# A transformer block on one core: late modulation columns summed on VectorE, two gates' products moved into the latent attention, rotary keys' low part on 128 rows

## The chip, the core and the metric

One Trainium2 chip, one of its cores. The metric is the device time of one execution in microseconds (us), the median of several runs. The engines are TensorE (PE: products into PSUM; PEld is its loading of weights), VectorE (DVE), ScalarE (ACT), GpSimd (POOL) and SyncE (SP), whose queue issues nearly all weight transfers. PSUM has eight banks of 128 x 512 floats.

## The reference

One layer on 256 latent rows `x` and 256 context rows, width 1024, all in float32. Cut to what matters here:

```python
m = silu(c) @ ada_w + ada_b                  # 6 x 1024 columns, split in six
h = rms_norm(x, g1) * (1 + m[1]) + m[0]
z = h @ w_in                                 # retention q, k, v, gate; latent cq, ckv, kr; gates g_ret, g_mla
att = softmax((q_nope @ k_nope + rope(q_rope) @ rope(k_rope)) * scale) @ v    # 8 heads
ret = bidirectional_retention(rope(q), rope(k), v)                            # 4 heads
r = head_rms(ret) * silu(ret_gate)
merged = sigmoid(g_ret) * (r @ w_branch_ret) + sigmoid(g_mla) * (att @ w_branch_mla)
x = x + m[2] * (merged @ w_out)
h2 = rms_norm(x, g2) * (1 + m[4]) + m[3]
x = x + m[5] * moe(h2)                       # top 4 of 32 experts, clamped SwiGLU
out = rms_norm(x, final_g)
```

`m[0]` and `m[1]` are needed at the start. The late modulation columns are `m[2]` to `m[5]`, 4096 columns of `ada_w`, needed only after the two branches are merged.

## The kernel before, in words

The program is a list of steps (`step`), which one Python pass turns into instructions in the order of the list; each engine takes its own in that order. A step may name a weight tile: 128 partitions x 1024 floats, 512 KB, loaded by SP into a ring of `WR` = 10 places, each refilled when it has been read. Most tiles are split into two float32r halves, high and low, in `split` (ScalarE copies, L276; VectorE subtracts, L277) `AHEAD` = 2 steps before their use, and a product is then three matmuls in `mm3` (L285 to L287). A raw tile is used as it is.

The stages in order: `ada_half` computes `m[0]`, `m[1]`; `modulate` gives the rows `hh`, `hl`; the latent projections; four pairs of heads of latent attention; `w_branch_mla`; four retention heads; the merge and `w_out`; the router; the experts. For each pair of heads the attention goes through `kv_up`, `scores` (the low part of the rotary keys, `krl`, has 64 rows, L700), the softmax on VectorE and ScalarE (L704 to L711), `attend_rows` (16 transposes, then four splits whose VectorE part is `ptl` and `kn`, L282), `q_rot` for the next pair, and `attend`. Between them stand steps that have work for TensorE meanwhile.

The late modulation columns are two quarters `q` of 2048 columns, eight steps `k` each (`ada_step`, L328 to L342). A step multiplies two raw tiles with a 128 x 32 stationary in four column groups; the first of a quarter also adds the bias (L296), and the bank of the quarter stays taken until its last step. Quarter 0 is spread over the attention by `FILL`, quarter 1 over the retention heads, two steps each. The gate columns of the attention (`C_GM + 512`) are four steps in pairs 1 to 3, the gate of a retention head (`C_RG + 512 * h`) four steps behind its scores. `gates` (L1154) spreads the sums over all rows for the residual and turns others into columns for the second modulation.

The expert weights, 192 transfers of 2 MB, pass through nine slots: three opened in `open_ring` in the last retention head, one in `close_early`, and at the end of the dense stage four rings (`add_ring(RINGS[2], ...)`) in the memory of `wr`, `wp` and `fk`, and one more, `halves`.

Of the kernel before, what the change touches and what calls it, by code (L numbers as in the profile page):

```python
# [21 lines left out]
TA = 512  # L22
# [7 lines left out]
RINGS = 3, 1, 4, 1  # L30
WR = 10
AHEAD = 2
FILL = 0, 1, 2, 1, 1, 1, 1, 1
MID = 4
# [25 lines left out]
def hybrid_block(ctx: ExitStack, tc: tile.TileContext, A, out, dbg=None):  # L60
# [21 lines left out]

    front = ExitStack()
    wr = [enter(front, f"wr{i}") for i in range(WR)]
    wp = [enter(front, f"wp{i}") for i in range(AHEAD + 1)]
    fk = enter(front, "fk")
    accp = enter(ctx, "accp", side="right")
# [17 lines left out]
    x0 = sp.tile([128, 4, D], F32, name="x0")  # L105
    adab = fk.tile([12, 512], F32, name="adab")
    dec = fk.tile([128, 2, RH], F32, name="dec")
# [30 lines left out]
    nc.vector.memset(magic, 0x5f3759df)  # L138
    pick = fk.tile([128, 128], F32, name="pick")
    nc.gpsimd.memset(pick, 0.0)  # L140
    for g in range(4):
        nc.gpsimd.memset(pick[32 * g:32 * g + 1], 1.0)
    slot = cst.tile([128, CAP], F32, name="slot")
# [38 lines left out]
    transpose(rp[:, 0:16], crow)  # L182
    sT = fk.tile([128, KD, 32], F32, name="sT")
    nc.vector.memset(sT, 0.0)
    nc.vector.tensor_copy(sT[:, :, 0:2], rp[:, 0:16].rearrange("p (r k) -> p k r", r=2))
    cols = fk.tile([128, 21], F32, name="cols")
# [15 lines left out]
    ada0 = sp.tile([128, 512], F32, name="ada0")  # L202
    ada = fk.tile([128, 2, 512], F32, name="ada")
    mod1 = fk.tile([128, 2, 2, KD], F32, name="mod1")
# [122 lines left out]

    def ada_step(q, k):  # L328

        for i in range(2):  # L330
            def f(w, i=i):
                if k == 0 and i == 0:
                    bank("ada")
                for c in range(2):
                    g = 2 * i + c
                    o = B["ada"][32 * g:32 * g + 32]
                    if k == 0:
                        ada_bias(o, 4 * (q + 1) + g)
                    nc.tensor.matmul(o, sT[:, k], w[:, 512 * c:512 * c + 512], start=False, stop=(k == KD - 1))  # L339
                if k == KD - 1 and i == 1:  # L340
                    nc.scalar.activation(ada[:, q], B["ada"], AF.Copy)
            step(f, (A["ada_w"][0], 128 * k, 1, [(2048 * (q + 1) + 1024 * i, 1024)], True))  # L342
# [60 lines left out]
    def whole(p):  # L403
        return p

    def project_lat(c0, names, kks=range(4)):
# [84 lines left out]
    def open_mla():  # L491
        dump("mod1", mod1)
        nc.sync.dma_start(tabm, A["tables"][:, 1024:1536])

        for q in range(4):
            nc.sync.dma_start(bgu[32 * q:32 * q + 32], A["exp_b_gu"][0, :, 512 * q:512 * q + 512])
        start.close()
        M["mp"] = enter(mla, "mp", reuse_waits="tile")
        M["mp2"] = enter(mla, "mp2", 2, reuse_waits="tile")
        mp = M["mp"]  # L500
        M["mT"] = [p.tile([128, MH, T], F32R, name="w") for p in first]
        M["cq"] = [mp.tile([128, 3, T], F32R, name=n) for n in ("cqh", "cql")]
        M["ck"] = [mp.tile([128, 2, TA], F32R, name=n) for n in ("ckh", "ckl")]
        M["krh"] = mp.tile([128, TA], F32R, name="krh")
        M["krl"] = mp.tile([64, TA], F32R, name="krl")
        M["acc"] = accp.tile([128, 2, D], F32, name="acc_m")
# [6 lines left out]
    def cq_norm():  # L513
        open_mla()
        mp = M["mp"]
# [172 lines left out]
    def scores(pair):  # L688
# [3 lines left out]
        for t in range(2):  # L692
# [48 lines left out]
    q_up(0, range(1, 3))  # L741
    npair = MH // 2
    for pair in range(npair):
        kv_up(pair)
# [6 lines left out]
        if pair == 1:  # L751
            q_up(1, range(2, 3))
            project_lat(C_GM + 512, ("gm0", "gm1"), range(1))
        if pair == 2:
            project_lat(C_GM + 512, ("gm0", "gm1"), range(1, 2))
        n = sum(FILL[:2 * pair])
        for k in range(FILL[2 * pair]):
            ada_step(0, n + k)
        if pair == 3:
            project_lat(C_GM + 512, ("gm0", "gm1"), range(2, 4))  # L760
            step(lambda: gate_mla_out(1))
# [43 lines left out]
    for c in range(2):  # L805
        step(lambda: bank("bm0", "bm1"))
        for k2 in range(4):
            matmul2(("bm0", "bm1"), "w_branch_mla", 256 * k2, 512 * c, lambda: M["mT"], 2 * k2, k2 == 0, k2 == 3)
        step(lambda c=c: branch_mla_out(c))

# [136 lines left out]

    def gate_out():
        sg = R["qe"].tile([128, 2, 512], F32, name="sg")
        for t in range(2):  # L950
            pg = B[("pg0", "pg1")[t]]
            tg = R["qe2"].tile([128, 512], F32, name="tg")
            nc.scalar.activation(tg, pg, AF.Tanh, scale=0.5)
            nc.vector.scalar_tensor_tensor(sg[:, t], tg, 1.0, pg, op0=OP.add, op1=OP.mult)
        R["sg"] = sg


# [17 lines left out]
    def ret_norm(h):  # L975
# [7 lines left out]
        for t in range(2):  # L983
            r = R["qp2"].tile([128, 512], F32, name="r")
            nc.vector.scalar_tensor_tensor(r, B[("po0", "po1")[t]], ro[:, t:t + 1], R["sg"][:, t],
                                           op0=OP.mult, op1=OP.mult)
# [16 lines left out]
    for h in range(RH):  # L1003
# [14 lines left out]
        else:  # L1018
# [20 lines left out]
        step(lambda: against_rows(1))  # L1039
        values(h, 0)  # L1040
        step(lambda: against_rows(2))
        values(h, 1)
        step(lambda: against_rows(3))
        if h == RH - 1:
# [109 lines left out]
    def gates():  # L1154
        mod2, rw, rbias = O["mod2"], O["rw"], O["rbias"]
        for i in range(2):
            s = slice(32 * i, 32 * i + 32)
            ps = pt_()
            nc.tensor.matmul(ps, pick[s], ada[s, 0], start=True, stop=True)
            nc.scalar.activation(O["gate1"][i], ps, AF.Copy)  # L1160
        ps = pt_()
        for i in range(2):
            s = slice(32 * (2 + i), 32 * (2 + i) + 32)
            nc.tensor.matmul(ps[64 * i:64 * i + 64], pick[s, 0:64], ada[s, 1], start=True, stop=True)
        nc.scalar.activation(O["gate2"], ps, AF.Copy)
        for q in (1, 0):
            pc = pt_((128, 4, 4, 32))
            for c in range(4):
                transpose(pc[:, c].rearrange("p a b -> p (a b)"), pairs(ada[:, q], 2)[:, c // 2, c % 2])
            for g in range(2):  # L1170
                if q == 1:
                    nc.vector.scalar_tensor_tensor(mod2[:, 0, 4 * g:4 * g + 4], pc[:, :, g, 0], 1.0,
                                                   g2c[:, 4 * g:4 * g + 4], op0=OP.add, op1=OP.mult)
                else:
                    nc.vector.tensor_copy(mod2[:, 1, 4 * g:4 * g + 4], pc[:, :, 2 + g, 0])

# [509 lines left out]
```

## Time and profile before

| | us |
|---|---|
| median of 3 runs | 1508.16 (1507.0 to 1508.19) |
| the profiled execution's own time | 1507.75 |
| its span, first to last instruction | 1506.0 |
| PE busy | 1414.9 (94%) |
| DVE busy | 613.6 (41%) |
| ACT busy | 345.8 (23%) |
| POOL busy | 77.0 (5%) |
| bytes moved | 492.38 MB, 327 GB/s over the span |

The page of the profile has the busy time of each engine, the span in 40 slices of 37.65 us, the chain of waits that ended last, and the costliest groups of instructions. The trace behind it is asked for single stretches, engines and lines. A busy TensorE says only that products follow each other, since they are pipelined: what one costs is read from the distance of two starts. An engine's idle time costs something only where another one waits for it.

### The profile page before, as it was taken

The numbers are of one execution on the slowest core, as the hardware profiler recorded it, in microseconds if no ns is written. First come the engines' busy times: TensorE is split into PE (matmuls) and PEld (weight loads), VectorE is DVE, ScalarE is ACT, GpSimd is POOL, SyncE is SP. The second block draws the span as 40 slices with busy tenths as digits, with TensorE's granted clock in tenths as the row PEclk, the third lists the DMA queues.
The fourth block names the chain that finished last, engine by engine and source line by source line (L and its number), as shares of the span: only waits on it lengthen the run. The fifth ranks groups of instructions, "written<-read, shape, count | busy, mean of one in ns | idle before, by whom it ended". The sixth has DMA issues, their size and how long they took to land.

```text
span 1506.0 us, 19151 instructions
## 1 busy us (share of the span) xinstructions
PE 1414.9 (94%) x7979; PEld 771.2 (51%) x7979; DVE 613.6 (41%) x1080; ACT 345.8 (23%) x606; POOL 77.0 (5%) x98
## 2 busy tenths in 40 slices
PE   8999999999999998999999999989899889998885
PEld 4676787888887884333333333333333333333323
DVE  4485645556576565232332323322232223223223
ACT  4363443444344341111010010110010001001101
POOL 2100040101010012000000000000000000000000
PEclk9999999999999999999999999999999999999998
DMA  9634363353546948999999999999999999999994
GB/s 319 203 109 144 140 227 108 128 192 112 182 126 210 352 166 369 426 426 427 426 428 425 429 425 427 428 425 429 426 427 426 428 427 428 426 427 427 427 422 178
DMA packets 75046, 492.38 MB, mean 327 GB/s; under 512 B 6563, under 2 KB 16860, under 8 KB 50120
## 3 DMA queue, kind: packets, MB, share of 16 engines
q1 hardware_dynamic: 74008, 489.22, 80.6%
q0 software_dynamic: 544, 1.21, 0.3%
q8 instruction: 64, 1.05, 0.3%
q10 hardware_dynamic: 400, 0.66, 0.1%
q14 instruction: 30, 0.25, 0.0%
HBM read 490.02 MB, written 1.05 MB: 326 GB/s over the span
## 4 chain that ended last, share of the span: by engine, by line
PE 55%; DMA 38%; DVE 5%; ACT 1%; issue 1%; POOL 0%; ACTq 0%; DVEq 0%; SPq 0%
DMA w<-in_exp_w_gu_dram 25%; DMA w<-in_exp_w_down_dram 13%; PE ps L1451 11%; PE ps L285 9%; PE ps L287 9%; PE ps L286 9%; PE ps L1482 5%; PE ps L149 3%; PE ps L1312 1%; PE ps L308 1%; PE ps L339 1%; PE ps L296 1%; PE ps L1431 1%; PE ps L437 1%; DVE up L1459 1%
## 5 line engine op out<-in xcount | busy, mean ns | idle before, releaser
L1451 PE MATMUL ps<-w,xg 128*64 128x512 f32 x2048 | 460.1, 596 | 38.1 <-DMA w<-in_exp_w_gu_dram 36.0
L1451 PEld LDWEIGHTS ps<-w,xg 128*64 128x64 f32 x2048 | 140.6, 137 | 336.0 <-issue 251.6
L1482 PE MATMUL ps<-w,ga 128*64 128x512 f32 x992 | 218.1, 592 | 0.0
L277 DVE TENSOR_TENSOR ws<-w,ws 128x1024 fp32r<-128x1024 f32 (+2 forms) x114 | 138.8, 1224 | 72.6 <-ACT ws L276 71.5
L1438 DVE SCALAR_TENSOR_TENSOR x<-ps,gate,x 128x512 f32<-128x512 f32 x124 | 84.5, 744 | 188.4 <-PE ps L1431 188.4
L1482 PEld LDWEIGHTS ps<-w,ga 128*64 128x64 f32 x992 | 71.3, 137 | 141.6 <-issue 141.6
L276 ACT ACTIVATE ws<-w 128x1024 fp32r<-128x1024 f32 (+2 forms) x114 | 116.9, 1027 | 94.5 <-PE ps L287 83.0
L1491 DVE TENSOR_TENSOR ps<-ps,gate 128x512 f32<-128x512 f32 (+1 forms) x33 | 22.5, 683 | 268.6 <-PE ps L1482 259.6
L1456 ACT ACTIVATE ps<-ga 128x512 f32<-128x512 f32 x32 | 19.3, 602 | 473.7 <-DVE ga L1455 473.7
L286 PE MATMUL ps<-ws,hh 128*128 128x512 f32 (+3 forms) x304 | 108.8, 358 | 3.2 <-DVE ws L277 3.2
L287 PE MATMUL ps<-ws,hl 128*128 128x512 f32 (+3 forms) x304 | 108.7, 357 | 0.7 <-DVE hl L384 0.7
L285 PE MATMUL ps<-ws,hh 128*128 128x512 f32 (+3 forms) x304 | 109.3, 360 | 0.0
L1455 DVE TENSOR_SCALAR ga<-ps 128x512 f32<-128x512 f32 x32 | 22.1, 691 | 162.4 <-PE ps L1451 162.4
L281 ACT ACTIVATE up<-ps 128x512 fp32r<-128x512 f32 (+1 forms) x33 | 19.3, 584 | 259.0 <-DVE ps L1491 258.9
L286 PEld LDWEIGHTS ps<-ws,hh 128*128 128x128 f32 x304 | 57.1, 188 | 12.8 <-DVE ws L277 4.6
L285 PEld LDWEIGHTS ps<-ws,hh 128*128 128x128 f32 x304 | 57.1, 188 | 12.7 <-issue 4.4
L1312 PE MATMUL ps<-bgu,ident 128*64 128x512 f32 x256 | 62.0, 605 | 0.0
L287 PEld LDWEIGHTS ps<-ws,hl 128*128 128x128 f32 x304 | 57.1, 188 | 8.5 <-DVE hl L384 1.0
L149 PE MATMUL ps<-ident,up 128*128 128x128 f32 x128 | 23.8, 308 | 22.9 <-DVE up L1459 22.9
L1398 PE MATMUL ps<-oh,acc_m 128*128 128x128 bf16 x512 | 40.1, 222 | 0.0
L1471 ACT ACTIVATE ga<-ps 128x512 f32<-128x512 f32 x32 | 19.1, 597 | 74.5 <-PE ps L149 74.5
L287 PE MATMUL ps<-ath,htl 128*128 128x256 f32 x128 | 35.8, 280 | 0.0
(382 smaller groups left out, 1812.2 us busy)
## 6 DMA issues: line engine op xcount, KB each, us to landing
w<-in_exp_w_gu_dram SPq DMA_DIRECT2D x124, 2048.0 KB, 39.1
w<-in_exp_w_down_dram SPq DMA_DIRECT2D x62, 2048.0 KB, 39.1
w<-in_ada_w_dram SPq DMA_DIRECT2D x48, 512.0 KB, 4.5
w<-in_w_in_dram SPq DMA_DIRECT2D x48, 512.0 KB, 4.7
w<-in_w_in_dram SPq DMA_DIRECT2D x32, 256.0 KB, 5.3
w<-in_w_branch_ret_dram SPq DMA_DIRECT2D x16, 512.0 KB, 5.4
w<-in_exp_w_gu_dram SPq DMA_DIRECT2D x8, 1024.0 KB, 27.1
w<-in_w_branch_mla_dram SPq DMA_DIRECT2D x8, 512.0 KB, 4.7
```

Of the source, the lines that this page charges most:

```text
L149: nc.tensor.transpose(dst, src, ident[:n, :n])
L276: nc.scalar.activation(hi[:, :n], src, AF.Copy)
L277: nc.vector.tensor_tensor(lo[:, :n], src, hi[:, :n].bitcast(F32), op=OP.subtract)
L285: nc.tensor.matmul(ps, a[0], b[0], start=start, stop=False, skip_group_check=True)
L286: nc.tensor.matmul(ps, a[0], b[1], start=False, stop=False, skip_group_check=True)
L287: nc.tensor.matmul(ps, a[1], b[0], start=False, stop=stop, skip_group_check=True)
L1312: nc.tensor.matmul(ps[64 * h:64 * h + 64], pick_row(c // 512).to_broadcast([128, CAP]), bgu, start=True, stop=False, skip_group_check=True)
L1398: nc.tensor.matmul(ps[:, i, :w], pairs(part[:, t], 4)[:, k // 2, k % 2], rhs, start=(t + p + i == 0), stop=(t + p == 3), skip_group_check= ...
L1438: nc.vector.scalar_tensor_tensor(a, pss[h], g[:, t:t + 1], a, op0=OP.mult, op1=OP.add)
L1451: nc.tensor.matmul(ps[64 * h:64 * h + 64], xg[k // 4][:, k % 4, sl], w[:, c:c + 512], start=False, stop=(k == KD - 1), skip_group_check=True)
L1482: nc.tensor.matmul(py[64 * h:64 * h + 64], hT[f], w[:, 1024 * r + 512 * h:1024 * r + 512 * h + 512], start=(f == 0), stop=(f == KD - 1))
L1491: nc.vector.tensor_tensor(py, py, gate2[:, cs], op=OP.mult)
```

## The change

The late modulation columns no longer use TensorE. `ada` is now 128 x 4096: cleared once, with the bias in row 0; for each raw tile one VectorE instruction adds the tile times the column `sc` of `silu(c)` (32 sums of 128 x 1024, `more_ada`). `gates` sums over the partitions with products with ones. The sums stand in the list behind the steps of the attention, the branch and the retention heads. In the attention the gate columns `C_GM + 512` and the first retention head's gate `C_RG` are now 16 pieces of six matmuls (`filler`), placed by the new `FILL`. The three other heads' gate has its first step ahead of the scores. `krl` has 128 rows. The ring has seven places, `fk` lies first in memory, and the last five expert slots are filled in another order.

```diff
-WR = 10
+WR = 7
-FILL = 0, 1, 2, 1, 1, 1, 1, 1
+FILL = 0, 2, 2, 2, 4, 2, 2, 2
-    def ada_step(q, k):
...
+    def ada_start():
+        nc.gpsimd.memset(ada, 0.0)
+        nc.gpsimd.dma_start(ada[0:1].rearrange("o q n -> o (q n)"), A["ada_b"][:, 2048:6144])
+
+    ada_todo = [(q, k, i) for q in range(2) for k in range(KD) for i in range(2)]
+
+    def more_ada(n):
+        for _ in range(n):
+            q, k, i = ada_todo.pop(0)
+
+            def f(w, q=q, k=k, i=i):
+                a = ada[:, q, 1024 * i:1024 * i + 1024]
+                nc.vector.scalar_tensor_tensor(a, w, sc[:, k:k + 1], a, op0=OP.mult, op1=OP.add)
             step(f, (A["ada_w"][0], 128 * k, 1, [(2048 * (q + 1) + 1024 * i, 1024)], True))
...
+    def filler(c0, names, done):
...
+            def f(*w):
+                if kk == 0:
+                    bank(*names)
+                if w:
+                    got["w"] = w
+                hi, lo = got["w"]
+                for t, n in enumerate(names):
+                    s = slice(128 * t, 128 * t + 128)
+                    mm3(B[n], (hh[:, kk, s], hl[:, kk, s]), (hi[:, k], lo[:, k]), start=(kk == 0), stop=(kk == KD - 1))
+            step(f, None if k else (A["w_in"][0], 128 * kk, 2, [(c0, 512)]))
...
-        nc.vector.tensor_tensor(M["krl"], ps[0:64], M["krh"][0:64].bitcast(F32), op=OP.subtract)
+        nc.vector.tensor_tensor(M["krl"], ps, M["krh"].bitcast(F32), op=OP.subtract)
...
-                nc.tensor.matmul(pss[i], q[0:64], M["krl"], start=False, stop=True, skip_group_check=True)
+                nc.tensor.matmul(pss[i], q, M["krl"], start=False, stop=True, skip_group_check=True)
...
+        fill(FILL[2 * pair])
+        more_ada(2)
         step(attend_rows)
         if pair + 1 < npair:
             step(lambda pair=pair: q_rot(pair + 1))
-        for k in range(FILL[2 * pair + 1]):
-            ada_step(0, n + FILL[2 * pair] + k)
+        fill(FILL[2 * pair + 1])
         step(lambda pair=pair: attend(pair))
+        more_ada(1)
...
-        ada_step(1, 2 * h)
+        if h:
+            project_lat(C_RG + 512 * h, ("pg0", "pg1"), range(1))
+        more_ada(1)
         step(ret_scores)
-        ada_step(1, 2 * h + 1)
-        project_lat(C_RG + 512 * h, ("pg0", "pg1"))
-        step(gate_out)
+        more_ada(1)
+        if h:
+            project_lat(C_RG + 512 * h, ("pg0", "pg1"), range(1, 4))
...
-    add_ring(RINGS[2], (1, 0, 2, 3, 4), halves)
+    add_ring(RINGS[2], (0, 2, 1, 3, 4), halves)
```

The remaining sums: one behind every second tile of `w_branch_mla`, and two among the values of each retention head.

How the instructions of three places stand in the built program (names as in the profile; lines are those of each version):

VectorE in pair 1, between the rotated queries (`tt`) and the splits of the attention weights (`ptl`, `kn`), which `attend` reads. Before:

```order
L620 TENSOR_TENSOR tt<-ta,tb 128x4x64
L277 TENSOR_TENSOR ws<-w_1387,ws 128x1024
L282 TENSOR_TENSOR ptl<-ps,pth 128x4x128 x2
L282 TENSOR_TENSOR kn<-ps,kn 128x4x128 x2
L659 TENSOR_TENSOR qr<-ps,qr 64x512
```

and now:

```order
L641 TENSOR_TENSOR tt<-ta,tb 128x4x64
L277 TENSOR_TENSOR ws<-w_1386,ws 128x1024
L340 SCALAR_TENSOR_TENSOR ada<-w_1234,sc,ada 128x1024
L340 SCALAR_TENSOR_TENSOR ada<-w_1237,sc,ada 128x1024
L282 TENSOR_TENSOR ptl<-ps,pth 128x4x128 x2
L282 TENSOR_TENSOR kn<-ps,kn 128x4x128 x2
L680 TENSOR_TENSOR qr<-ps,qr 64x512
```

Two sums (L340) stand ahead of the four subtractions; it is so in each of the four pairs.

VectorE in the first retention head, around the scores (L944 before, L976 now, then the low parts `atl`). Before:

```order
L843 CAST htl<-ps 128x4x128 x2
L944 SCALAR_TENSOR_TENSOR ra<-ps,w 128x512
L282 TENSOR_TENSOR atl<-ra,ath 128x512
L944 SCALAR_TENSOR_TENSOR ra<-ps,w 128x512
L282 TENSOR_TENSOR atl<-ra,ath 128x512
L277 TENSOR_TENSOR ws<-w_2269,ws 128x1024
```

and now:

```order
L875 CAST htl<-ps 128x4x128 x2
L340 SCALAR_TENSOR_TENSOR ada<-w_2229,sc,ada 128x1024
L976 SCALAR_TENSOR_TENSOR ra<-ps,w 128x512
L282 TENSOR_TENSOR atl<-ra,ath 128x512
L976 SCALAR_TENSOR_TENSOR ra<-ps,w 128x512
L282 TENSOR_TENSOR atl<-ra,ath 128x512
L340 SCALAR_TENSOR_TENSOR ada<-w_2246,sc,ada 128x1024
L282 TENSOR_TENSOR gtl<-ps,gth 128x512 x2
```

A sum stands on either side of the scores, and the splits of the gate's tiles that followed are gone, since its products are in the attention now.

The SP queue from the ring's opening (three expert tiles) to the last slots. Before:

```order
L267 DMA w_4592<-in_w_out_dram 128x2x512
L267 DMA w_4609<-in_w_out_dram 128x2x512
L1075 DMA w<-in_exp_w_gu_dram 128x4096 x3
L267 DMA w_4714<-in_w_out_dram 128x2x512
L267 DMA w_4760<-in_w_out_dram 128x2x512
L267 DMA w_4821<-in_w_out_dram 128x2x512
L267 DMA w_4838<-in_w_out_dram 128x2x512
L1075 DMA w<-in_exp_w_gu_dram 128x4096
L267 DMA w_4950<-in_w_out_dram 128x2x512
L267 DMA w_4967<-in_w_out_dram 128x2x512
L1080 DMA w<-in_exp_w_down_dram 128x4096 x2
```

and now:

```order
L1107 DMA w<-in_exp_w_gu_dram 128x4096
L267 DMA w_4894<-in_w_out_dram 128x2x512
L267 DMA w_4911<-in_w_out_dram 128x2x512
L267 DMA w_4934<-in_w_out_dram 128x2x512
L267 DMA w_4951<-in_w_out_dram 128x2x512
L267 DMA w_4995<-in_w_out_dram 128x2x512
L1112 DMA w<-in_exp_w_down_dram 128x4096 x2
```

Five tiles of `w_out` instead of two stand between the fourth expert tile and the last five.

## Rows read from the trace of the kernel before

**Rows 1.** The page, 40 slices of 37.65 us: TensorE's busy tenths, memory traffic.
```profile
PE   8999999999999998999999999989899889998885
...
GB/s 319 203 109 144 140 227 108 128 192 112 182 126 210 352 166 369 426 426 427 426 428 425 429 425 427 428 425 429 426 427 426 428 427 428 426 427 427 427 422 178
```

**Rows 2.** Chain of waits, first expert product and end: start us, us, what.
```profile
579.90 7.02 PE ps L1451 x32
...
904.39 37.93 DMA w<-in_exp_w_gu_dram
```

**Rows 3.** Stretches: PE, PEld, DVE, ACT, POOL busy (x), granted clock, DMA share, GB/s.
```profile
100.00:200.00 100.00, 99.30 (x554) 70.40 (x553) 65.77 (x132) 46.57 (x89) 7.15 (x15) 1.00 0.42 138
...
525.00:530.00 5.00, 5.00 (x23) 4.01 (x22) 3.54 (x5) 2.13 (x2) 0.00 (x0) 1.00 0.04 14
...
580.00:585.00 5.00, 5.00 (x24) 1.61 (x24) 1.48 (x5) 1.15 (x3) 0.00 (x0) 1.00 0.31 67
```

**Rows 4.** Timeline of SP's queue, the fifth and sixth expert tile.
```profile
541.47 11.91 SPq L1080 DMA_DIRECT2D w<-in_exp_w_down_dram  x2
```

**Rows 5.** Timeline of TensorE, pairs 0 and 1: start us, us, line, [idle before <-releaser].
```profile
111.57 0.60 PE L149 MATMUL ps<-ident,tt 128*128 128x128 f32 x4
112.10 1.04 PE L296 MATMUL ps<-adab,ident 12*32 12x512 f32 x2
...
145.14 0.35 PE L285 MATMUL ps<-pth,mvh 128*128 128x256 f32 x1 [0.25 <-DVE ptl L282]
```

**Rows 6.** Chain of waits, late modulation: a bias piece, and a step in pair 3.
```profile
112.17 0.97 PE ps L296 x2
...
182.15 1.00 PE ps L339 x8
```

**Rows 7.** Timeline of TensorE, a group of rotary products in the scores of pair 1.
```profile
129.63 0.40 PE L287 MATMUL ps<-kn,qnl 128*128 128x512 f32 x1
129.86 0.39 PE L699 MATMUL ps<-krh,qr 128*128 128x512 f32 x1
130.18 0.49 PE L700 MATMUL ps<-krl,qr 64*128 64x512 f32 x1
...
131.45 0.50 PE L285 MATMUL ps<-kn,qnh 128*128 128x512 f32 x1
```

**Rows 8.** Groups by line, VectorE, 95 to 240 us: xcount | busy us, mean ns | idle before.
```profile
L277 DVE TENSOR_TENSOR ws<-w,ws 128x1024 fp32r<-128x1024 f32 x21 | 26.4, 1257 | 21.0 <-ACT ws L276 21.0
...
L803 DVE SCALAR_TENSOR_TENSOR acc_m<-acc_m,ps 128x512 f32<-128x512 f32 x4 | 2.6, 680 | 0.0
```

**Rows 9.** Timeline of VectorE in pairs 0, 1 and 3.
```profile
108.71 2.09 DVE L277 TENSOR_TENSOR ws<-w,ws 128x1024 fp32r<-128x1024 f32 x2
...
144.31 1.27 DVE L282 TENSOR_TENSOR ptl<-ps,pth 128x512 fp32r<-128x512 f32 x2
...
184.96 0.49 DVE L711 TENSOR_SCALAR t2k<-t2k,smx 128x512 f32<-128x512 f32 x1
```

**Rows 10.** Timeline of VectorE, the first retention head's scores.
```profile
241.70 1.28 DVE L843 CAST htl<-ps 128x512 fp32r<-128x512 f32 x2
251.29 0.69 DVE L944 SCALAR_TENSOR_TENSOR ra<-ps,w 128x512 f32<-128x512 f32 x1 [8.31 <-PE ps L287]
...
254.68 0.69 DVE L282 TENSOR_TENSOR atl<-ra,ath 128x512 fp32r<-128x512 f32 x1 [0.70 <-ACT ath L281]
```

**Rows 11.** Timeline of TensorE, the gate rows and what follows.
```profile
515.30 1.13 PE L1159 MATMUL ps<-ada,pick 32*128 32x512 f32 x4
...
519.38 1.28 PE L149 MATMUL ps<-ident,r 128*128 128x128 f32 x8 [0.79 <-DVE r L985]
520.50 1.87 PE L1182 MATMUL ps<-ct,mod 128*128 128x32 f32 x16
```

**Rows 12.** The page, transfers: KB each, median us from issue to landing.
```profile
w<-in_ada_w_dram SPq DMA_DIRECT2D x48, 512.0 KB, 4.5
```

**Rows 13.** Timeline of GpSimd, the clear of a small tile at the start.
```profile
4.74 0.22 POOL L140 MEMSET pick<- 128x128 f32 x1
```

More of the change, by code (lines that the diff above doesn't have):

```diff
@@ L83, in hybrid_block @@
     front = ExitStack()
+    fk = enter(front, "fk")
     wr = [enter(front, f"wr{i}") for i in range(WR)]
     wp = [enter(front, f"wp{i}") for i in range(AHEAD + 1)]
-    fk = enter(front, "fk")
     accp = enter(ctx, "accp", side="right")
@@ L105, in hybrid_block @@
     x0 = sp.tile([128, 4, D], F32, name="x0")
-    adab = fk.tile([12, 512], F32, name="adab")
+    adab = sp.tile([12, 512], F32, name="adab")
     dec = fk.tile([128, 2, RH], F32, name="dec")
@@ L138, in hybrid_block @@
     nc.vector.memset(magic, 0x5f3759df)
[L139 to L142, printed above, removed]
     slot = cst.tile([128, CAP], F32, name="slot")
@@ L182, in hybrid_block @@
     transpose(rp[:, 0:16], crow)
-    sT = fk.tile([128, KD, 32], F32, name="sT")
+    sT = sp.tile([128, KD, 32], F32, name="sT")
+    sc = fk.tile([128, KD], F32, name="sc")
     nc.vector.memset(sT, 0.0)
+    nc.vector.tensor_copy(sc, rp[:, 0:KD])
     nc.vector.tensor_copy(sT[:, :, 0:2], rp[:, 0:16].rearrange("p (r k) -> p k r", r=2))
@@ L202, in hybrid_block @@
     ada0 = sp.tile([128, 512], F32, name="ada0")
-    ada = fk.tile([128, 2, 512], F32, name="ada")
+    ada = fk.tile([128, 2, 2048], F32, name="ada")
     mod1 = fk.tile([128, 2, 2, KD], F32, name="mod1")
@@ L404, in whole, with piece @@
         return p
+    def filler(c0, names, done):
+        got = {}
+        def piece(kk):
+            k = kk % 2
+            def f(*w):
[8 more added lines that the diff above has]
+            step(f, None if k else (A["w_in"][0], 128 * kk, 2, [(c0, 512)]))
+            if kk == KD - 1:
+                step(done)
+        return [lambda kk=kk: piece(kk) for kk in range(KD)]
     def project_lat(c0, names, kks=range(4)):
@@ L504, in open_mla @@
         M["krh"] = mp.tile([128, TA], F32R, name="krh")
-        M["krl"] = mp.tile([64, TA], F32R, name="krl")
+        M["krl"] = mp.tile([128, TA], F32R, name="krl")
         M["acc"] = accp.tile([128, 2, D], F32, name="acc_m")
@@ L514, in cq_norm @@
         open_mla()
+        ada_start()
         mp = M["mp"]
@@ L742, in hybrid_block, with gate_out, fill @@
     npair = MH // 2
+    sg0 = fk.tile([128, 2, 512], F32, name="sg0")
+    def gate_out(sg, tmp):
+        for t in range(2):
+            pg = B[("pg0", "pg1")[t]]
+            tg = tmp()
+            nc.scalar.activation(tg, pg, AF.Tanh, scale=0.5)
+            nc.vector.scalar_tensor_tensor(sg[:, t], tg, 1.0, pg, op0=OP.add, op1=OP.mult)
+    fills = (filler(C_GM + 512, ("gm0", "gm1"), lambda: gate_mla_out(1)) +
+             filler(C_RG, ("pg0", "pg1"), lambda: gate_out(sg0, lambda: t2k([128, 512]))))
+    def fill(n):
+        for _ in range(n):
+            fills.pop(0)()
     for pair in range(npair):
@@ L752, in hybrid_block @@
             q_up(1, range(2, 3))
[L753 to L761, printed above, removed]
+        fill(FILL[2 * pair])
+        more_ada(2)
         step(attend_rows)
@@ L946, in ret_scores @@
         R["at"] = ath, atl
[L948 to L955, printed above, removed]
     def against_rows(q):
@@ L1026, in hybrid_block, with gate_head @@
             branch(h - 1, 1, add_branch(h - 1))
-        ada_step(1, 2 * h)
+        if h:
+            project_lat(C_RG + 512 * h, ("pg0", "pg1"), range(1))
+        more_ada(1)
         step(ret_scores)
-        ada_step(1, 2 * h + 1)
-        project_lat(C_RG + 512 * h, ("pg0", "pg1"))
-        step(gate_out)
+        more_ada(1)
+        if h:
+            project_lat(C_RG + 512 * h, ("pg0", "pg1"), range(1, 4))
+            def gate_head():
+                R["sg"] = R["qe"].tile([128, 2, 512], F32, name="sg")
+                gate_out(R["sg"], lambda: R["qe2"].tile([128, 512], F32, name="tg"))
+            step(gate_head)
         if h == RH - 1:
@@ L1154, in gates @@
     def gates():
-        mod2, rw, rbias = O["mod2"], O["rw"], O["rbias"]
+        mod2 = O["mod2"]
         for i in range(2):
-            s = slice(32 * i, 32 * i + 32)
             ps = pt_()
-            nc.tensor.matmul(ps, pick[s], ada[s, 0], start=True, stop=True)
+            nc.tensor.matmul(ps, one32[:, 0:1].to_broadcast([128, 128]), ada[:, 0, 512 * i:512 * i + 512],
+                             start=True, stop=True)
             nc.scalar.activation(O["gate1"][i], ps, AF.Copy)
@@ L1162, in gates @@
         for i in range(2):
-            s = slice(32 * (2 + i), 32 * (2 + i) + 32)
-            nc.tensor.matmul(ps[64 * i:64 * i + 64], pick[s, 0:64], ada[s, 1], start=True, stop=True)
+            nc.tensor.matmul(ps[64 * i:64 * i + 64], one32[:, 0:1].to_broadcast([128, 64]),
+                             ada[:, 1, 1024 + 512 * i:1536 + 512 * i], start=True, stop=True)
         nc.scalar.activation(O["gate2"], ps, AF.Copy)
[L1166 to L1175, printed above, removed]
+        pc = pt_((128, 2, KD))
+        for i, part in enumerate((ada[:, 1, 0:1024], ada[:, 0, 1024:2048])):
+            for k in range(KD):
+                nc.tensor.matmul(pc[:, i, k:k + 1], pairs(part, 4)[:, k // 2, k % 2], one32[:, 0:1], start=True, stop=True)
+        nc.vector.scalar_tensor_tensor(mod2[:, 0], pc[:, 0], 1.0, g2c, op0=OP.add, op1=OP.mult)
+        nc.vector.tensor_copy(mod2[:, 1], pc[:, 1])
     def router_weights():
```

17 lines of the change are left out of this document (4 added, 13 removed).

## The prediction

> **What bounds the kernel now.** I read the page's slices first [rows 1]. The PE digits are 9 from the fourth slice to the fourteenth, and in these slices the memory moves 108 to 227 GB/s; from slice 17 on it is 422 to 430 GB/s to the end. So there are two stages: a dense one, up to some 560 us, that TensorE fills, and the experts, which the loading of their weights fills. The chain of waits shows how the two are joined [rows 2]: it goes along TensorE to the first expert product at 579.90, on along TensorE, and from 904.39 to the end over weight transfers of some 39 us each. The expert weights lie in nine slots of 2 MB. The stretches of 5 us show the transfers at 4% of their capacity at 525 and at 31% from 580 to 585 [rows 3]: they wait for a slot, first for one that the dense stage still holds (the SP queue gets to the fifth tile at 541.47 [rows 4]), then, with all nine full, for the first expert to give one back. So the stream of weights starts when the first expert's products start, and runs at its rate from there. A microsecond less of TensorE's work before 560 us starts the experts a microsecond earlier and ends the kernel a microsecond earlier. That is what I price.
>
> In the hundred microseconds of the latent attention TensorE is busy for 99.3, VectorE for 65.8 [rows 3]; the one wait of TensorE between the head pairs is 0.25 us at 145.14 [rows 5]. There every removed product counts in full, and every new wait too.
>
> **The sum.** Durations are from the profiled execution, 1507.75 us; the median of the runs is 0.4 above it.
>
> *Products removed.* The late modulation's sixteen steps (two quarters of eight) leave TensorE. A step after the first takes 1.00 us [rows 6]; there are 14: 14.0. The first step of a quarter adds the bias, and there bias and product take turns without overlap: eight pieces of 0.97 [rows 6], 7.8; two of them, 15.6. Together **29.6 us**, all on the path.
>
> *128 rows.* In the scores two of four products have a low part of 64 rows. The products of 128 rows on either side start 0.23 apart; the four, from 129.86 to 131.45, take 1.59 [rows 7]. At 0.23 each they would take 0.93. Each score half has one such group, two per pair, eight in all: 8 x 0.66 = **5.3 us**. The VectorE subtraction for the low part gets twice the rows and the same columns; I cost it at nothing, as it is one instruction.
>
> *Products moved.* The two gates' products are the same 96, of 512 columns. A piece is six, 1.4 us at 0.23; sixteen pieces. No cost by themselves; what matters is which wait they cover.
>
> *Sums added on VectorE.* 32 sums of 128x1024 in place of the products. The nearest rows are the split of a 128x1024 tile, 1.26 mean, 2.09 for two in a row [rows 8, 9], and a sum of half the length, 0.68 [rows 8]: 1.05 to 1.36 each, I take 1.15, the same length from the same memory; 37 us over some 350. VectorE has room for that on the average [rows 3]. What counts is where a sum stands in front of something that TensorE needs soon. VectorE takes its instructions in order, and in each of the four head pairs two sums (2.3) now stand before the four subtractions that the attention products wait for.
> - Pair 0: the splits end at 108.71 + 2.09 = 110.80 [rows 9]. With the sums, and some 0.3 for scores that end earlier against VectorE, the first subtraction ends at 114.1. TensorE is through its transposes at 112.10 [rows 5], and goes on with gate pieces; these write a bank that this first subtraction frees. Wait **2.0**.
> - Pair 1: attention already waited 0.25 for the subtractions [rows 5], which end at 144.31 + 1.27 [rows 9]. Now they come 2.3 later, and TensorE gets there some 0.5 earlier (three steps of 1.00 out, two pieces of 1.4 in, shorter scores). Added wait **2.8**.
> - Pair 2: six pieces, 8.4, stand where 2.8 + 2.0 stood. This covers the sums: 0, at most 1.
> - Pair 3: scores end at 182.15 [rows 6]; two pieces, the transposes (16 at 0.13 [rows 5], 2.1) and two pieces more end 7.7 later, at 189.85. VectorE's last division ends at 185.45 [rows 9]; then 0.3, a split 1.2 [rows 8], the sums 2.3, two subtractions 1.3: 190.6. Wait **0.8**.
>
> *The first retention head.* It loses both of its covers: the first step with its bias ahead of the scores, and the gate's projection (48 products, 11 us) behind them. The chain from the first score to the last low part takes VectorE and ScalarE from 251.29 to 255.37 [rows 10]. Before it now stand the last two copies of the rows, 241.70 to 242.98 [rows 10], and a sum. TensorE's transposes end about as these copies start, and its 24 products of 256 columns (half of 0.23 each) then take 2.8, up to 244.5; six more need only the first half (0.7). On VectorE, in the same times, the sum ends at 244.1 and the chain at 248.2; less 244.5 and 0.7 that is 3.0. Wait **3.0**, bounds 1.5 (the sum gets into an idle moment) and 4 (a second sum or a late tile before it).
>
> *The four gate rows.* From 515.30 to 519.38 TensorE has the old form and then waits for the normalized rows [rows 11]. The new form has two products on all rows (0.97 each by [rows 6]), two on half the columns side by side (1.0), and 16 products of one column, which are 32 instructions. The nearest row is 16 instructions of 32 columns in 1.87, 0.117 each [rows 11]: 3.7. Together 6.6 against 4.1: **2.5**, bounds 0 and 4. The Trainium skill, TensorEngine Tiling (Array Packing), Instruction Overhead, says that a product of one column costs as much as one of 60, about 60 cycles. By that the 32 would take an estimated 0.8 instead of 3.7, the four gate rows would cost nothing, and the sum would be 2.5 lower.
>
> *Loads.* The ring of weight tiles has seven places, not ten, and some of them now wait for a sum on VectorE before the SP queue may refill them; the queue stands still behind such a place. Two tiles are split ahead, so a load has some four tiles of lead, 11 us at 2.8 per tile; where a sum stands after every two tiles, about 7.5. Landing takes 4.5 [rows 12]. I take 0; where the ring of experts loads beside it, a wait of 3 in all is the upper bound. Clearing the sums' target, 32 times the 0.22 of the small clear [rows 13], is 7 us on GpSimd some 40 us ahead of the first sum: 0; if it stopped VectorE altogether, up to 7, which I do not take into the range.
>
> Sum: 29.6 + 5.3 = 34.9 off; 2.0 + 2.8 + 0 + 0.8 + 3.0 + 2.5 = 11.1 on. Net 23.8 off: 1484.0 against the profiled execution, **1484.4** against the median.
>
> **The rivals.**
> - *VectorE keeps up.* The sums fall into its idle moments, and only the gate rows cost: 34.9 - 2.5 = 32.4 off, 1475.8. For it: VectorE is idle a third of this stretch [rows 3]. Against it: the order puts the sums right ahead of the subtractions. 0.08.
> - *VectorE becomes the bound of the attention.* The waits are twice as long, since one late subtraction also makes the next pair's splits late: 22.2 on, 12.7 off, 1495.5. For it: pair 1 was late before the change. Against it: with three sums more per pair VectorE still has some 20 of 100 us left [rows 3], in which it gets even after a pair. 0.14.
> - *The transfers set the end anyway.* If the start of the stream did not hang on TensorE, nothing would move: 1508. Against it speak the pauses in [rows 3]. 0.04.
> - *The experts' slots fill too late, slower.* The last five tiles stand in the memory of the ring, the sums and the weight copies. Before, the transfers were through with them just when the first expert started. The dense stage now gets shorter, and five projections of the output stand in the SP queue between the fourth expert tile and these five, where there were two. Each late tile costs 2 MB at 427 GB/s [rows 1], 4.9. All five late are 24.6, which eats the 23.8, and the experts then wait for their own weights: 1509 to 1512. It decides from 24 us of lateness on. Against it: the first of the five now waits only for the gate rows, so it can go some 10 us earlier than at 541.47. 0.04.
>
> **How the numbers follow.** The sum as it stands gets 0.70. Its own bounds: with half of the attention's waits (2.8), 1.5 for the head and nothing for the gate rows, 30.6 off, 1477.6; with waits of 10, 4, 4 and 3 for the loads, 13.9 off, 1494.3, and the second rival lies there too. Range 1478 to 1496, which leaves out the first rival, no change and slower, 0.16. About 0.2%, 3 us, is what a measurement can tell: faster 0.70 + 0.08 + 0.14 = 0.92, same 0.04, slower 0.04.
>
> **What would show it.** The first expert's products start near 556; TensorE's new waits in the dense stage are named VectorE, on the gate pieces of pair 0, the attention products of pairs 1 and 3, and the first head's products with the rows; between two score products of any kind lie 0.23. The first of the five late tiles goes out before 530. I am wrong if the wait for a weight copy or for a transfer appears in TensorE's list before 550, or if the pause of the transfers at the first expert is gone.

## The result, and the profile after

The changed kernel takes **1492.16 us** (median of four runs, 1487.58 to 1494.40), the kernel before 1507.58 in the same session (1505.83 to 1508.19). The ratio is 0.9896, 95% interval 0.9882 to 0.9911: 15.4 us faster. The forecast, 1484.4 with a range of 1478 to 1496, holds the time and the direction; 7.8 us of the 23.8 that it promised are missing. The profiled run took 1487.58 (span 1485.8), so about half of what is missing lies in that trace, and half in how the other runs differ from it.

The joint of the two stages is where the prediction had it. In the chain of waits after the change the first expert's products start at

```profile
559.65 7.02 PE ps L1479 x32
```

20.25 earlier than in [rows 2], and the span is 20.2 shorter. In every trace below, the span ends 926.0 to 926.4 us after this point, so I follow TensorE's lead to there and no further. The late tiles were in time. The timeline of SP's queue has the first two of the five at

```profile
511.73 17.86 SPq L1112 DMA_DIRECT2D w<-in_exp_w_down_dram  x2
```

ahead of 530, where [rows 4] has 541.47, and the transfers still pause at the first expert (25% of their capacity from 560 to 565 us). TensorE's timeline after the change, at the places of the prediction (start, us, line, in brackets the idle time before and its releaser):

```profile
100.01 0.40 PE L721 MATMUL ps<-krl,qr 128*128 128x512 f32 x1
100.24 0.40 PE L720 MATMUL ps<-krh,qr 128*128 128x512 f32 x1
...
109.06 0.60 PE L145 MATMUL ps<-ident,tt 128*128 128x128 f32 x4
112.11 0.50 PE L285 MATMUL ps<-ws,hh 128*128 128x512 f32 x1 [2.44 <-DVE ptl L282]
...
127.27 0.50 PE L285 MATMUL ps<-kn,qnh 128*128 128x512 f32 x1 [0.63 <-ACT t2k L728]
...
142.93 0.58 PE L286 MATMUL ps<-ptl,mvh 128*128 128x256 f32 x1 [2.93 <-DVE ptl L282]
143.31 0.41 PE L287 MATMUL ps<-pth,mvl 128*128 128x256 f32 x1
...
189.47 0.39 PE L286 MATMUL ps<-ptl,mvh 128*128 128x256 f32 x1 [0.82 <-DVE ptl L282]
...
243.61 0.38 PE L285 MATMUL ps<-ath,hth 128*128 128x256 f32 x1 [0.79 <-ACT ath L281]
244.35 0.38 PE L286 MATMUL ps<-atl,hth 128*128 128x256 f32 x1 [0.36 <-DVE atl L282]
245.62 0.38 PE L285 MATMUL ps<-ath,hth 128*128 128x256 f32 x1 [0.41 <-ACT ath L281]
246.34 0.38 PE L286 MATMUL ps<-atl,hth 128*128 128x256 f32 x1 [0.34 <-DVE atl L282]
```

The rotary products stand 0.23 apart, which [rows 7] did not have for the low part. The waits of pairs 0, 1 and 3 are at the instructions that were named; of the head's four, the two for `ath` (1.20 us together) are named ScalarE and not VectorE. VectorE's timeline shows what stands ahead of pair 1's subtractions, and the group of the sums what one costs:

```profile
137.52 1.76 DVE L277 TENSOR_TENSOR ws<-w,ws 128x1024 fp32r<-128x1024 f32 x1
139.20 2.47 DVE L340 SCALAR_TENSOR_TENSOR ada<-w,sc,ada 128x1024 f32<-128x1024 f32 x2
141.59 1.28 DVE L282 TENSOR_TENSOR ptl<-ps,pth 128x512 fp32r<-128x512 f32 x2
```
```profile
L340 DVE SCALAR_TENSOR_TENSOR ada<-w,sc,ada 128x1024 f32<-128x1024 f32 x32 | 40.6, 1278 | 0.0
```

What the prediction does not have is in the spacing of the products. Those of 256 columns behind the wait of 2.93 start 0.21 apart, where the same kind takes 0.12 elsewhere. At the gate rows it is plainer:

```profile
487.98 1.88 PE L1190 MATMUL ps<-ada,one 128*128 128x512 f32 x4
489.78 1.08 PE L1195 MATMUL ps<-ada,one 128*64 128x512 f32 x4
490.79 4.47 PE L1201 MATMUL ps<-one,ada 128*128 128x1 f32 x32
495.12 1.95 PE L145 MATMUL ps<-ident,r 128*128 128x128 f32 x8
496.86 3.46 PE L1210 MATMUL ps<-ct,mod 128*128 128x32 f32 x16
500.13 0.77 PE L285 MATMUL ps<-ws,ath 128*128 128x512 f32 x1
500.70 0.63 PE L286 MATMUL ps<-ws,ath 128*128 128x512 f32 x1
```

The transposes of r take 1.95, the router's products 3.46 and a branch product 0.63, where [rows 11] has 1.28 and 1.87 for the first two. The stretches of 2 us say why (busy time by engine, then TensorE's granted clock, DMA share, GB/s):

```profile
144.00:146.00 2.00, 2.00 (x12) 2.00 (x12) 1.94 (x3) 0.32 (x1) 0.00 (x0) 0.56 0.81 254
...
494.00:496.00 2.00, 2.00 (x11) 2.00 (x11) 0.24 (x2) 0.00 (x0) 0.00 (x0) 0.50 1.01 429
...
500.00:502.00 2.00, 2.00 (x7) 1.61 (x7) 1.64 (x3) 0.00 (x0) 0.00 (x0) 0.50 0.07 27
```

TensorE runs at half its clock (1.2 GHz of 2.4) from some 494 to 504 us and from about 142.5 to 145.7. Before the change the same places ran at 1.00:

```profile
140.00:150.00 10.00, 9.60 (x75) 6.86 (x68) 8.23 (x16) 4.26 (x8) 3.40 (x5) 1.00 0.81 254
500.00:525.00 25.00, 24.18 (x142) 19.60 (x141) 13.12 (x34) 9.43 (x16) 2.15 (x3) 1.00 0.96 369
```

### The profile page after: what moved, and what is told of

Same layout as the page of the kernel before. It is cut to its first block, busy times and chain, and to the rows that moved or that the text cites. A ratio compares the mean times of both kernels' runs of the same rounds, so it can differ in the third digit from the quotient of the medians.

```text
span 1485.8 us, 18943 instructions
## 1 busy us (share of the span) xinstructions
PE 1388.0 (93%) x7859; PEld 775.8 (52%) x7859; DVE 651.5 (44%) x1111; ACT 344.4 (23%) x604; POOL 87.9 (6%) x95
## 3 DMA queue, kind: packets, MB, share of 16 engines
q0 software_dynamic: 576, 1.23, 0.3%
## 4 chain that ended last, share of the span: by engine, by line
PE 51%; DMA 40%; DVE 6%; issue 1%; ACT 1%; POOL 0%; SPq 0%; DVEq 0%; ACTq 0%
DMA w<-in_exp_w_gu_dram 26%; DMA w<-in_exp_w_down_dram 13%; PE ps L1479 11%; PE ps L286 9%; PE ps L287 9%; PE ps L285 9%; PE ps L1510 5%; PE ps L145 2%; PE ps L1340 1%; PE ps L308 1%; PE ps L1459 1%; PE ps L457 1%; DVE up L1487 1%; DVE up L1485 1%; DVE ws L277 0%
## 5 line engine op out<-in xcount | busy, mean ns | idle before, releaser
L340 DVE SCALAR_TENSOR_TENSOR ada<-w,sc,ada 128x1024 f32<-128x1024 f32 x32 | 40.6, 1278 | 0.0
L285 PE MATMUL ps<-ath,hth 128*128 128x256 f32 x128 | 35.7, 279 | 1.2 <-ACT ath L281 1.2
```

Source lines behind the costliest of these rows:

```text
L285: nc.tensor.matmul(ps, a[0], b[0], start=start, stop=False, skip_group_check=True)
L340: nc.vector.scalar_tensor_tensor(a, w, sc[:, k:k + 1], a, op0=OP.mult, op1=OP.add)
```

## The experiments

Theory 1: the terms were priced about right, and what is missing is TensorE's clock, at the gate rows in each run and behind some of the new waits. Theory 2, the rival: VectorE's sums take it, by their length and by what they delay. "The changed kernel" below is 1492.0, the median of eight runs (1487.58 to 1494.40).

**The sums put apart.**

```diff
-        more_ada(2)
         step(attend_rows)
...
-        step(lambda pair=pair: attend(pair))
+        for i in range(2):
+            more_ada(1)
+            step(lambda pair=pair, i=i: attend(pair, (i,)))
         more_ada(1)
```

> The changed kernel with the three sums of each head pair put apart: one ahead of the attention products of the first head, one between the two heads, one behind; none ahead of the four subtractions. Theory 1 (waits priced about right, the shortfall lies at the gate rows and in the granted clock there): the waits of TensorE for ptl, 2.4, 2.9 and 0.8 us, go, and with the one of 2.9 the low granted clock of 140 to 148 us (about 1 us more), so 6 to 7 us off, about 1485.5; the granted clock of 0.50 at the gate rows and what it costs stay as they are. Theory 2 (VectorE's sums are the shortfall, 1.28 us each and not 1.15, and the clock falls only because TensorE waited before): the lead at the gate rows grows by more than these three waits, 8 us and over, and the low clock at the gate rows gets shorter too.

1484.46 us (ratio to before 0.9853, 0.9837 to 0.9870): 7.5 off by the medians, between the figures of the two theories. The waits for `ptl`, 6.1 us in the first trace, are down to one of 0.5, no stretch of the attention is under 1.00, and the low clock at the gate rows, which by theory 2 gets shorter, lasts even longer (489 to 504 us): theory 1. TensorE's list of waits (us in total, times, longest), and a stretch there:

```profile
PE ps L286 <- DVE ws L277: 2.9, 3, 1.5
...
PE ps L286 <- DVE ptl L282: 0.5, 1, 0.5
PE ps L286 <- DVE kn L282: 0.5, 1, 0.5
```
```profile
490.00:492.00 2.00, 2.00 (x11) 2.00 (x11) 0.00 (x0) 0.00 (x0) 0.00 (x0) 0.50 1.03 438
```

At their new places the sums bring short waits of their own: 0.5 for `kn` and 0.8 more for a weight split (`ws`) than the 2.1 that the changed kernel and the one before it have. So trace against trace the gain is smaller than between the medians: from the first pair's first product (`ckh`) to the first head's first product with the rows (`ath`) it takes 147.15 us, where the first trace of the changed kernel has 151.87 and its three others (below) 152.14 to 154.83.

**The sums cut to 32 columns.**

```diff
-                a = ada[:, q, 1024 * i:1024 * i + 1024]
-                nc.vector.scalar_tensor_tensor(a, w, sc[:, k:k + 1], a, ...
+                a = ada[:, q, 1024 * i:1024 * i + 32]
+                nc.vector.scalar_tensor_tensor(a, w[:, 0:32], sc[:, k:k + 1], a, ...
```

> The changed kernel with each of the 32 sums cut to 32 of its 1024 columns (the rest of the late modulation is left out); loads, places and waits are as they are. What it loses in time is what VectorE's sums cost in all. Theory 1 (the sums cost the waits seen in TensorE's list and the low clock behind them, and the apart-put sums have shown nearly all of it): 7 to 9 us below the changed kernel, 1483 to 1485, the half clock at the gate rows stays. Theory 2 (the sums also cost by what they take from transfers and from other engines' memory ports): 1480 or lower.

1481.22 us (1479.42 to 1482.95), 10.8 off, between the two. The trace shows 4.8 us less of waits for `ptl`, 0.8 less in the first head, and no low clock before the gate rows, which costs the changed kernel 1.3 to 6.0 us a run (below): 7 to 12 together. Trace against trace it is tighter: from the first pair's start to the first expert it takes 461.21 us where the first trace of the changed kernel takes 467.90, 6.7 off, and the waits with that trace's 1.3 of half clock account for 6.9. That leaves theory 2 no part that it is needed for.

**The one-column products put apart**, four groups of four products between the value products of the last head.

```diff
+        gate_cols(h, 1, 0)
         step(lambda: against_rows(2))
         values(h, 1)
         more_ada(1)
+        gate_cols(h, 1, 4)
         step(lambda: against_rows(3))
...
+        gate_cols(h, 0, 0)
         values(h, 2)
+        gate_cols(h, 0, 4)
         values(h, 3)
```

> The changed kernel with the 16 one-column products in four groups of four (8 instructions, about 1.1 us each) between the value products of the last retention head; the 512-column products of the gate rows stay where they are. Theory 1: the granted clock stays at 1.00 from 480 to 505 us, the stretch from the last value product to the first branch product falls from 12.1 us by the 4.5 of the moved group and some 2 us of half clock, plus 1.6 us in the branch products behind it, minus the 4 us that the moved group now takes elsewhere: 4 to 5 us off, about 1487.5, and the runs lie closer together than the 7 us of the changed kernel. Theory 2: the clock falls there all the same (the transposes and the router's products do it), the wait of 0.8 us for the normalized rows comes back, and the time is within 1.5 us of the changed kernel.

The profiled run is the fastest, 1484.87; the three others are at 1490 (median 1490.00). The trace shows the gate rows as theory 1 has them:

```profile
488.86 0.99 PE L1032 MATMUL ps<-one,ada 128*128 128x1 f32 x8
492.57 1.88 PE L1208 MATMUL ps<-ada,one 128*128 128x512 f32 x4
494.38 1.08 PE L1213 MATMUL ps<-ada,one 128*64 128x512 f32 x4
496.75 1.29 PE L145 MATMUL ps<-ident,r 128*128 128x128 f32 x8 [1.29 <-DVE r L1008]
497.87 1.87 PE L1222 MATMUL ps<-ct,mod 128*128 128x32 f32 x16
```
```profile
480.00:512.00 32.00, 30.43 (x168) 24.65 (x167) 18.79 (x40) 12.26 (x19) 2.17 (x3) 1.00 0.81 283
```

The first view is the timeline, the second the stretch from 480 to 512 us: the clock is 1.00 throughout. From the last head's first product with the rows to the last branch product it takes 44.1 us, the changed kernel 47.1: 3.0 off, with the wait for r back at 1.29; between the medians it is 2.0. The expectation that the runs draw together was wrong: they still differ by 5.3 us, so that comes from elsewhere.

**The changed kernel again**, three more traces.

> The changed kernel once more, for a second trace and five more times. Its runs lay between 1487.6 and 1494.4 us where those of the kernel before lay within 2.4. Theory 1: what differs between its runs is where and how long the granted clock is low; this trace has the same waits for VectorE within 0.3 us, and a difference to the first trace lies in stretches with a clock under 1.00. Theory 2: the difference lies in the waits for VectorE or for a transfer, with the same clock.

> The changed kernel, one look, to catch a run of the longer bunch (1491 to 1494 us at a mean clock of 0.984 to 0.987). Theory 1 (several of the waits at pair 0, pair 1 and the first retention head are followed by half clock in such a run, where the shorter runs have one): a run over 1491 shows two or three such stretches in the attention or the first head. Theory 2: it shows one there, and another stretch elsewhere before 560 us.

> The changed kernel, a second look, as the one before it: by theory 1 the time follows the number and the length of the stretches of half clock before 560 us, about 1.5 to 3 us each, with the waits themselves the same within 0.3 us; by theory 2 it doesn't.

The traced runs took 1488.90, 1493.75 and 1488.49 us, with waits equal to the first trace's within 0.1. The first and the third have one short stretch of half clock, behind pair 0's wait. The long one has three, behind pair 0, pair 1 and the first head:

```profile
114.00:116.00 2.00, 2.00 (x7) 1.59 (x6) 1.94 (x4) 0.00 (x0) 0.00 (x0) 0.52 0.91 320
...
146.00:148.00 2.00, 2.00 (x11) 2.00 (x11) 1.94 (x4) 0.00 (x0) 0.00 (x0) 0.50 0.94 301
148.00:150.00 2.00, 2.00 (x11) 2.00 (x11) 1.24 (x2) 0.39 (x1) 0.00 (x0) 0.50 0.73 251
...
252.00:254.00 2.00, 2.00 (x11) 2.00 (x10) 0.00 (x0) 0.00 (x0) 0.00 (x0) 0.50 0.53 151
```

Against the same products at 1.00 they cost 1.6, 2.7 and 1.7 us, 6.0 together; the first trace's one, behind pair 1, costs 1.3. The difference, 4.7, and a start that is 1.2 later when the first pair begins (92.95 against 91.75; 91.75 to 92.95 over the four) make 5.9 of the 6.2 us between the two runs. That is theory 1.

**64 rows again**, first in the changed kernel, then with both groups put apart.

```diff
-        M["krl"] = mp.tile([128, TA], F32R, name="krl")
+        M["krl"] = mp.tile([64, TA], F32R, name="krl")
...
-                nc.tensor.matmul(pss[i], q, M["krl"], ...
+                nc.tensor.matmul(pss[i], q[0:64], M["krl"], ...
```

> The changed kernel with the rotary keys' low part back at 64 rows; all else as changed. Both theories: the four rotary products of a score group take 1.6 us again where they now take 0.93, eight groups, so 5 to 6 us longer than the changed kernel (1492.2), about 1498; the list of TensorE's waits in the attention stays, since VectorE's chain starts behind the scores and moves with them. If a part of the 5.3 had been hidden behind the new waits for VectorE, the loss would be below 3.

> The sums and the gate columns put apart, and the low part of the rotary keys at 64 rows. In the first test of the 64 rows the median rose by only 1 us, though its first expert started 5.3 us later than in the trace of the changed kernel; its runs all had a clock of 0.988 and lay within 2 us, the changed kernel's lay in two bunches. Theory 1 (the bunches hid the price): without the waits for VectorE the runs are close together, and the 64 rows cost 5 to 6 us against the kernel with the first two edits. Theory 2 (the longer scores give VectorE the time that its sums take, so that most of the price is won back): 1 to 2.5 us.

The first gave 1492.53 us, only 0.5 lost by the medians; but one short stretch of low clock in its trace stands against one to three in the changed kernel's, so the medians hide the price. The second gave 1484.69 against 1480.95 without the 64 rows: **3.7 us**, between the theories. The traces agree. The four pairs' scores are 5.8 us shorter with 128 rows, not counting waits; but the stretch from pair 0 to the first head's scores is only 3.2 us shorter, since with the shorter scores TensorE waits 0.6 for the bank that ScalarE's exponential reads, 0.6 for `qnl` (the low half of the next pair's queries) and 0.8 for a weight split, which make 2.0 of the 2.6 and none of which the 64 rows show. The trace with 64 rows also has half clock behind the first head (244 to 248 us), which the other has not; between the first two heads' first products with the rows it takes 69.79 us for 68.26. So a part of the 3.7 may be that.

**The first retention head**: the last transposes of the rows and the sum behind the scores.

```diff
             step(qk_rows)
-            step(lambda: rows_back(range(6, KD)))
...
-        more_ada(1)
+        if h:
+            more_ada(1)
         step(ret_scores)
+        if h == 0:
+            step(lambda: rows_back(range(6, KD)))
+            more_ada(1)
         more_ada(1)
```

> The changed kernel with the edit of the first retention head alone. Theory 1: the waits there fall from 1.9 us to under 1; 1 to 1.5 us off in a run with the same granted clock. Theory 2: the waits only move to the scores, which stand closer behind their own transposes; nothing gained.

1487.54 us (1484.81 to 1490.07), 4.5 below the changed kernel's median, more than expected. The four waits of 1.9 fall to 1.0, and the fastest run lies 2.8 below the changed kernel's fastest; how much of the rest is the low clock that no longer follows there, the runs are too few to say. Its profiled run, the longest, again has half clock behind pairs 0 and 1 (1.6 and 2.7 us).

**The edits together.**

> Both edits together: the three sums of a pair put apart (1484.5 alone) and the one-column products put apart (1484.9 and 1490 alone). The traces so far show one short stretch of half clock, 3 to 4 us, behind one of the waits of the attention or of the first retention head, another one in each run, and 10 to 12 us of it at the gate rows. Theory 1 (each wait or burst has its own stretch of half clock, and the longer runs of the changed kernel, 1491 to 1494, have a further one behind the waits in the attention): the gains add, about 1480.5, runs within 2 us. Theory 2 (the longer runs come from a place that neither edit touches): the fastest run is at 1480.5, but others stay 4 to 6 us above it.

1480.95 us (1478.91 to 1481.34): 11.1 off, where the edits alone gave 7.5 and 2.0; the runs lie within 2.4 us, and the trace has a clock of 1.00 from 0 to 540 us. The spread goes when the waits in the attention go: theory 1. The longer runs of the gate edit alone have no trace; that theirs came from the same place follows only from their absence here.

> The same, and in the first retention head the last transposes of the rows and the sum stand behind the scores, not ahead of them. Theory 1: the four waits of 1.9 us together in that head shrink to under 1, and no stretch of half clock follows there: 1 to 2.5 us below the kernel with the first two edits, about 1479. Theory 2 (the head's chain over VectorE and ScalarE is as long wherever the sum stands; its length was 4.1 us before the change): the waits stay at 1.5 to 2 us and the time stays the same within 0.5.

**1477.62 us** (1477.27 to 1481.19; ratio to before 0.9813, 0.9800 to 0.9827), the best of all: 14.4 below the changed kernel by the medians, 3.3 below the one with two edits. Between these two the runs overlap, and trace against trace, from the first pair's start to the first expert, it is 1.1 (458.37 against 459.45), about what the four waits lose. That is theory 1 at its lower end. The first expert starts at

```profile
549.79 7.02 PE ps L1495 x32
```

and the gate rows' stretch is at full clock:

```profile
476.00:508.00 32.00, 30.38 (x162) 24.09 (x161) 19.00 (x42) 13.13 (x19) 2.17 (x3) 1.00 0.82 288
```

**The last group back at the gate rows**, as a cover for the wait for r: `gate_cols(RH - 1, 0, 4)` behind `gates()`.

> The kernel with all three edits (1477.6), the last of the four groups of one-column products back behind the 512-column products of the gate rows, where TensorE waits 1.3 us for the normalized rows. Theory 1 (eight such instructions, 0.85 us, are too few to bring the clock down): the wait falls to 0.4, 0.9 us off, about 1476.7. Theory 2 (any of them next to the transposes and the router's products does): half clock at the gate rows again, 2 to 4 us longer.

1480.65 us (1478.12 to 1482.93), 3.0 longer by the medians; but the runs overlap, and from the first pair's start to the first expert the trace is only 0.55 longer (458.92 against 458.37). The wait falls to 0.25, and half clock behind it takes back more than that: theory 2 in kind, with less than its 2 to 4 us shown. In this trace eight instructions of one column next to the others are enough:

```profile
492.00:494.00 2.00, 2.00 (x10) 1.81 (x10) 1.29 (x4) 0.60 (x1) 0.00 (x0) 0.56 0.95 382
494.00:496.00 2.00, 2.00 (x7) 1.57 (x6) 0.76 (x1) 0.00 (x0) 0.00 (x0) 0.58 0.80 287
```

## Why the prediction was right, and where it was short

The direction and the mechanism held: removed products count in full up to the first expert, and the span follows one for one. The rivals fell: VectorE neither kept up (1475.8) nor became the bound (its waits are those of the sum, 9.4 us with the restarts behind them, and pair 2 has none), and no tile came late. The time alone does not tell the second rival from the forecast, only the waits do: it doubled all 11.1, the gate rows included; with only the 8.6 of VectorE's waits doubled it would have stood at 1493.0, next to the median. In [rows 1] two figures were read loosely, and nothing hung on them: the fourteenth slice has 352 GB/s, and from slice 17 on it is 422 to 429 and 178 in the last. Term by term in the profiled run, us:

| term | forecast | measured, by how much the stage got longer |
|---|---|---|
| 128 rows, off | 5.3 | 5.8, four score stages |
| pair 0, 1, 2, 3 | 2.0, 2.8, 0, 0.8 | 2.7, 2.8, 0, 1.1 |
| next waits in line, pair 1 | 0 | 0.9 (bank) + 0.7 (`qnl`) |
| first retention head | 3.0 | 2.8 |
| gate rows | 2.5, bounds 0 and 4 | 5.2, and 1.6 in the branch products behind |
| half clock behind pair 1's wait | not priced | 1.3 |

A stage gets longer by more than the idle time in TensorE's timeline (2.44 in pair 0, 1.9 in the head), since products start up again behind each wait.

- *Sums.* 1.28 each, not 1.15; two in a row 2.47, for which the sum had 2.3. The waits came out within 0.7 all the same.
- *128 rows.* The products were priced right, but nothing was costed for what becomes late next. With 64 and 128 rows side by side, 3.2 to 3.7 of the 5.8 are left.
- **The step that failed is the gate rows: 6.8 for 2.5.** I costed each instruction by a row at full clock and asked only for its length. The length was right: put apart, eight one-column instructions take 0.85 to the next product, 0.107 each, 3.4 for the 32 (forecast 3.7). Each of them loads weights of 128 columns, and in the burst these loads (PEld) are busy for 2.00 of the 2 us from 492 to 494; that fits a price which is nearly the same for 1 column and for 32 (0.117), but no run varies the loads. What was wrong is that such a burst leaves what follows at full clock. It halves the clock for some 10 us, and 3.0 of the 6.8 us come back when the burst is put apart. The Trainium skill, TensorEngine Tiling (Array Packing), Instruction Overhead, by which the 32 would have taken an estimated 0.8, is not borne out: in a row they took 4.3, partly at half clock, and at the pace of the groups put apart 3.4.
- **The waits were priced by their length alone.** Behind them come 1.3 to 6.0 us of half clock, differing from run to run, which is why the median lies 4.6 above the profiled run. The clock of 1.00 in the attention [rows 3] I took as given after the change too.

With the table's numbers, 29.6 + 5.8 off and 19.1 on make 16.3 for the profiled run, which has 20.25. These other 3.9 no term forecast, and without them the run would have stood at about 1491.5: that it came within 3.6 of its forecast is luck. Of them, TensorE was 0.95 ahead before the first pair, within what the start varies by; some 1.1 is in products of the attention that stand a little closer (a pair's attention products take 2.86 where they took 2.96); and about 1.8 is in the retention heads: between the first products with the rows of heads 1 and 2 the time fell from 68.70 to 66.02, for two steps of 1.00. That 66.02 is the same within 0.01 in all thirteen traces after the change, the one with the cut sums among them. Products of 256 columns are there 0.113 apart where they were 0.118, for a reason that I did not test.

## What to carry to other kernels

Where TensorE is the path, ask of each new wait, and of each run of tiny products, what the granted clock will be behind it: here one burst of 32 one-column instructions of 3.4 us cost 3.0 more in half clock, and waits of 2 to 3 us drew up to 6 us more. Put added work of another engine behind the instructions that TensorE needs next, one at a time, and scatter small products among dense ones. When runs of one kernel fall apart by several us, trace more than one of them before reading a median.

## What the runs showed of the hardware

- The granted clock fell to 0.50 with TensorE counted busy. In the eight traces with the 32 one-column instructions in a row it did each time, for about 10 us (in one about 14); in the four with groups of eight between dense products never; in the one with the last eight next to the 512-column products, the transposes and the router's products, it did, for 3 to 4 us.
- Behind a wait it fell in some runs only: behind pair 0's 2.4 us in five traces of six, behind pair 1's 2.9 us in three of seven, behind the first head's four short waits of 1.9 together in three of nine. It stayed low for some 3 to 7 us, though TensorE had dense products again at once. Behind the router's wait of 5.2 us (for `selb`, just ahead of the first expert) it fell in all fourteen traces, the kernel's before among them (0.50 from 572 to 578 us), so that stretch is no part of the loss. What decides it behind the shorter waits stays open.
- VectorE's split of a 128x1024 tile at 137.52, in the chain to pair 1's wait, took 1.76 us where [rows 8] has 1.26 in the mean. It is no part of the loss: the kernel before has the same 1.76 there (at 142.63). In the traces before and after, the 159 splits of this shape without a GpSimd instruction beside them took 1.21 to 1.23, and the twelve that took 1.39 or more each had one beside them (up to 2.32); but others with one beside them took 1.22 too. No run here takes GpSimd's work away.
